# Gate and up projections as seven block products of 256 tokens, the gated product kept in float32 until the down projection, the norm factor of up applied behind it

## The chip, the core and the metric

The kernel runs on one core of a Trainium2 chip. That core has a matrix engine (TensorE, PE in the rows; its weight loads stand apart as PEld), VectorE (DVE), ScalarE (ACT), GpSimd (POOL), a queue engine that issues transfers (SyncE, SP), and sixteen DMA engines. What counts is device time of one call in microseconds; lower is better. TensorE has two clock levels, 1.2 and 2.4 GHz; the profile gives the granted clock as a share of the higher one.

## The reference

One layer of a hybrid encoder on 512 tokens of width 1024 with 16 meta tokens: two attention branches, merged and projected, then a SwiGLU block, then a last norm. Only the second half matters here:

```
x = x + merged @ w_o
h = rmsnorm(x, ffn_norm)
x = x + (jax.nn.silu(h @ w_gate) * (h @ w_up)) @ w_down
h = rmsnorm(x, final_norm)
return h[:, N_META:]
```

`w_gate` and `w_up` are 1024 x 2816, `w_down` is 2816 x 1024, all float32. The norm divides each token by the root of its mean square, so its factor is one number per token and can be applied after a projection as well as before it.

## The kernel before

Features lie on the 128 partitions, tokens along the free axis: `x1` is 8 tiles of 128 features by 512 tokens. A float32 product is made of three matmuls (`mm3`): every operand is split into a high part in float32r (a cast on ScalarE) and the rest (a subtraction on VectorE), and high x high, high x low and low x high are added up in PSUM. Each matmul has a 128x128 weight tile and 512 tokens, and each has its own weight load.

The last part of the program, `phase_b`, has these stages on TensorE, one after the other without barriers:

- `pn` (32 x 3 matmuls), the attention branch that is left, and the merge; `po` (64 x 3), the output projection, whose result is added to `x1`, scaled by the norm's weight and split into `xgh`, `xgl`;
- gate and up: 22 passes, one for each block f of 128 of the 2816 columns. A pass runs 8 x 3 matmuls for gate and 8 x 3 for up, and then `glu` (lines 971 to 979): VectorE multiplies gate by the norm factor R2, ScalarE applies silu, VectorE multiplies up by R2 and the two with each other, and the product is split at once into `gh[:, f]`, `gl[:, f]`. The sum of squares that R2 needs is complete only when the stage begins, so its small matmuls (`ms`, line 183) and the matmul that spreads it over the partitions (`rp`, line 886) stand in passes 0 and 1;
- down: 8 output blocks m, each 22 x 3 matmuls (`pdn`) over all blocks of `gh`, `gl`. The last block is done in two halves of 256 tokens (`pdh`, line 919), so that the final norm and the store of one half run beside the other.

Weights come in pieces of 512 KB in the order of `wplan`; `wnext` (line 124) keeps up to four pieces loaded and up to two split. `wraw` has three buffers, `whi` and `wlo` two each. The order on each engine is not the order of the text: a scheduler lists the instructions by readiness under a model of their cost, and each engine then works through its list strictly in that order, waiting on semaphores.

Of the kernel before, what the change touches and what calls it, by code (L numbers as in the profile page):

```python
# [10 lines left out]
F32 = mybir.dt.float32  # L11
# [23 lines left out]
NF = D_FF // P  # L35
EPS = 1e-6
# [32 lines left out]
class Kernel:  # L69
# [9 lines left out]
    def wplan(self):  # L79
# [58 lines left out]
    def mm3(self, outs, wh, wl, rhs, start, stop):  # L138
        nc = self.nc
        n = len(outs)  # L140
        for i in range(n):
            nc.tensor.matmul(outs[i], wh, rhs[i][0], start=start, stop=False)  # L142
        for i in range(n):
            nc.tensor.matmul(outs[i], wh, rhs[i][1], start=False, stop=False)  # L144
        for i in range(n):
            nc.tensor.matmul(outs[i], wl, rhs[i][0], start=False, stop=stop)  # L146
# [662 lines left out]
    def phase_b(self, sA2):  # L809
        tc, nc, a = self.tc, self.nc, self.a  # L810
        with ExitStack() as top:
            self.pjp = top.enter_context(tc.tile_pool(name="pjb", bufs=8, space=PSUM))
            X = top.enter_context(tc.tile_pool(name="X", bufs=1, side="right"))
            x1 = X.tile([P, KT, T], F32, name="x1")
            bt = top.enter_context(tc.tile_pool(name="bt", bufs=1, side="right"))
            sX = ExitStack()
            XG = sX.enter_context(tc.tile_pool(name="XG", bufs=1, side="right"))
            xgh = XG.tile([P, KT, T], F32R, name="xgh")
            xgl = XG.tile([P, KT, T], F32R, name="xgl")
            for m in range(KT):  # L820
                nc.gpsimd.dma_start(x1[:, m], a["x"][m][:, :T])
            sM = ExitStack()
            M = sM.enter_context(tc.tile_pool(name="M", bufs=1))
            mh = M.tile([P, KT, T], F32R, name="mh")
            ml = M.tile([P, KT, T], F32R, name="ml")
            m2 = self.m2
            for m in range(KT):
# [12 lines left out]
                self.split(mh[:, m], ml[:, m], m2[:, m])  # L840


            ssq = bt.tile([P, T], F32, name="ssq2", tag="ssq", bufs=1)
            for m in range(KT):
                wh, wl = self.wnext()
                po = self.pj("po")
                for k in range(KT):
                    self.mm3([po], wh[:, k], wl[:, k], [(mh[:, k], ml[:, k])], k == 0, k == KT - 1)
                nc.vector.tensor_tensor(out=x1[:, m], in0=x1[:, m], in1=po, op=ALU.add)
                nc.scalar.activation(xgh[:, m], x1[:, m], AF.Copy, scale=self.g2[:, m:m + 1])  # L850
                nc.vector.scalar_tensor_tensor(out=xgl[:, m], in0=x1[:, m], scalar=self.g2[:, m:m + 1],
                                               in1=xgh[:, m].bitcast(F32), op0=ALU.mult, op1=ALU.subtract)
                self.sum_sq(bt, ssq, x1[:, m], m, KT)
            sM.close()
            sA2.close()


            sG = ExitStack()
            G = sG.enter_context(tc.tile_pool(name="G", bufs=1))
            gh = G.tile([P, NF, T], F32R, name="gh")  # L860
            gl = G.tile([P, NF, T], F32R, name="gl")
            R2 = bt.tile([P, T], F32, name="R2")
            held = []
            for f in range(NF):
                pgu = []
                for j in range(2):
                    wh, wl = self.wnext()
                    ps = self.pj("pf")
                    for k in range(KT):
                        self.mm3([ps], wh[:, k], wl[:, k], [(xgh[:, k], xgl[:, k])], k == 0, k == KT - 1)  # L870
                        if f == 0 and j == 1 and k < 4:
                            if k == 0:
                                ms = self.pj("ms2")
                                msg = self.mean_sq(ms, ssq, P, 4, self.ones_d)
                            next(msg)
                    pgu.append(ps)
                if f == 0:
                    y = self.rsqrt(ms[:, 0:4], EPS)
                    dg = bt.tile([P, T], F32, name="dg", tag="t0", bufs=3)
                    self.diag(dg.rearrange("p (c q) -> p c q", c=4), y, P, 4)  # L880
                held.append((f, pgu))
                if f == 0:
                    continue
# [4 lines left out]
                while held:  # L888
                    self.glu(bt, R2, gh, gl, *held.pop(0))
# [180 lines left out]
```

## Time and profile before

| | us |
|---|---|
| median of three runs (lowest, highest) | 783.49 (781.88, 784.15) |
| the profiled execution | 784.85 |
| its span, first to last instruction | 783.1 |
| gate and up, first matmul to the first of down (408.47 to 649.69) | 241.2 |
| down, without its last block (649.69 to 754.41) | 104.7 |
| last block of down | 18 |
| behind the last matmul of down | 10.6 |

The profile is one execution. TensorE's busy time is the union of its matmuls' durations; each duration contains the time that a matmul takes to drain, which overlaps with the next one, so the duration of one (391 ns) is longer than the spacing of two starts. Spacings are read from starts.

### The profile page before, as it was taken

To read this page: it belongs to the slowest core of one execution; us is meant where nothing else is said; L and a number is where in the kernel's file an instruction comes from. 1 tells how busy PE (TensorE), PEld (TensorE's weight loads), DVE (VectorE), ACT (ScalarE), POOL (GpSimd) and SP (SyncE) were. 2 spreads that over 40 slices of the span, in tenths; PEclk is the share of its full clock that TensorE was granted. 3 is DMA by queue.
4 is the path that set the end of the run, shared out by engine and by line. 5 is a ranking of instruction groups with operands and counts; after the bars stand their busy time and mean duration, and the time that the engine had idled before them with its cause. 6 is when DMAs were issued, how large, how long until landed. Compare 5 with 4: busy or idle time off the path is not lost.

```text
span 783.1 us, 10564 instructions
## 1 busy us (share of the span) xinstructions
PE 768.4 (98%) x4002; PEld 654.0 (84%) x4002; DVE 457.5 (58%) x888; ACT 310.4 (40%) x522; POOL 58.3 (7%) x141
## 2 busy tenths in 40 slices
PE   7999999999999999999999999999999999999995
PEld 5899889989999888878888888888888888888884
DVE  5778898798788866657453644444444445222314
ACT  6246555555545547424341523223232233222311
POOL 2030110110011000020220000000000000000100
PEclk8999999999999999999999999999999999999997
DMA  7474644444463411353323222323323235332313
GB/s 261 130 193 130 167 117 110 128 124 129 113 170 107 107 70 63 100 185 111 104 84 108 81 100 88 108 87 101 100 89 108 88 94 173 104 95 78 108 37 107
DMA packets 31970, 89.20 MB, mean 114 GB/s; under 512 B 4208, under 2 KB 6272, under 8 KB 31920
## 3 DMA queue, kind: packets, MB, share of 16 engines
q1 hardware_dynamic: 29952, 84.41, 35.5%
q0 software_dynamic: 1136, 3.34, 1.5%
q10 hardware_dynamic: 832, 0.79, 0.3%
q8 instruction: 31, 0.51, 0.3%
q14 instruction: 19, 0.16, 0.1%
HBM read 71.45 MB, written 2.10 MB: 94 GB/s over the span
## 4 chain that ended last, share of the span: by engine, by line
PE 92%; DVE 4%; DMA 2%; SPq 1%; issue 1%; ACT 0%; DVEq 0%; ACTq 0%
PE pf L142 10%; PE pf L144 10%; PE pf L146 10%; PE pdn L146 4%; PE pdn L142 4%; PE pdn L144 4%; PE pg L142 4%; PE pg L144 4%; PE pg L146 4%; PE s L515 2%; PE po L146 2%; PE po L144 2%; PE po L142 2%; PE pq L142 2%; PE pq L144 2%; PE pq L146 2%
## 5 line engine op out<-in xcount | busy, mean ns | idle before, releaser
L119 ACT CAST whi<-wraw 128x1024 fp32r<-128x1024 f32 (+2 forms) x123 | 126.9, 1032 | 297.4 <-issue 108.3
L120 DVE TENSOR_TENSOR wlo<-wraw,whi 128x1024 fp32r<-128x1024 f32 (+2 forms) x123 | 147.4, 1198 | 91.7 <-ACT whi L119 87.1
L142 PE MATMUL pf<-xgh,whi 128*128 128x512 f32 x352 | 137.7, 391 | 0.0
L144 PE MATMUL pf<-xgl,whi 128*128 128x512 f32 x352 | 137.0, 389 | 0.0
L146 PE MATMUL pf<-xgh,wlo 128*128 128x512 f32 x352 | 137.0, 389 | 0.0
L142 PEld LDWEIGHTS pf<-xgh,whi 128*128 128x128 f32 x352 | 66.1, 188 | 13.9 <-issue 0.2
L146 PEld LDWEIGHTS pf<-xgh,wlo 128*128 128x128 f32 x352 | 66.1, 188 | 13.9
L144 PEld LDWEIGHTS pf<-xgl,whi 128*128 128x128 f32 x352 | 66.1, 188 | 13.6 <-issue 0.2
L142 PE MATMUL pdn<-gh,whi 128*128 128x512 f32 x154 | 59.9, 389 | 0.0
L144 PE MATMUL pdn<-gl,whi 128*128 128x512 f32 x154 | 59.9, 389 | 0.0
L146 PE MATMUL pdn<-gh,wlo 128*128 128x512 f32 x154 | 59.9, 389 | 0.0
L977 DVE TENSOR_TENSOR u<-pf,R 128x512 f32<-128x512 f32 x22 | 15.2, 691 | 65.6 <-PE pf L146 65.6
L142 PE MATMUL pg<-xh,whi 128*128 128x512 f32 x128 | 52.7, 411 | 0.4 <-DVE vt L381 0.4
L144 PE MATMUL pg<-xl,whi 128*128 128x512 f32 x128 | 50.6, 396 | 0.0
L146 PE MATMUL pg<-xh,wlo 128*128 128x512 f32 x128 | 50.2, 392 | 0.0
L989 POOL TENSOR_TENSOR ssq<-ssq,sq 128x512 f32<-128x512 f32 x11 | 19.4, 1761 | 376.5 <-ACT sq L988 376.5
L975 DVE TENSOR_TENSOR s<-pf,R 128x512 f32<-128x512 f32 x22 | 15.2, 690 | 42.1 <-PE pf L146 42.1
L156 ACT CAST ath<-tp 128x256 fp32r<-128x256 f32 (+1 forms) x48 | 20.5, 443 | 42.3 <-PE tp L639 22.0
L146 PEld LDWEIGHTS pdn<-gh,wlo 128*128 128x128 f32 x154 | 28.9, 188 | 6.1
L144 PEld LDWEIGHTS pdn<-gl,whi 128*128 128x128 f32 x154 | 28.9, 188 | 6.1
L142 PEld LDWEIGHTS pdn<-gh,whi 128*128 128x128 f32 x154 | 28.9, 188 | 5.9
L142 PE MATMUL pk<-xh,whi 128*128 128x256 f32 (+1 forms) x128 | 29.2, 306 | 2.7 <-ACT xh L246 2.7
(222 smaller groups left out, 1497.9 us busy)
## 6 DMA issues: line engine op xcount, KB each, us to landing
wraw<-in_w_in_dram SPq DMA_DIRECT2D x39, 512.0 KB, 3.5
wraw<-in_w_gate_dram SPq DMA_DIRECT2D x22, 512.0 KB, 3.2
wraw<-in_w_up_dram SPq DMA_DIRECT2D x22, 512.0 KB, 3.2
kd<-khl SPq DMA_DIRECT2D x32, 264.0 KB, 4.1
wraw<-in_w_down_dram SPq DMA_DIRECT2D x16, 512.0 KB, 3.5
qs<-qhl SPq DMA_DIRECT2D x32, 128.0 KB, 2.9
wraw<-in_w_o_dram SPq DMA_DIRECT2D x8, 512.0 KB, 3.3
wraw<-in_w_down_dram SPq DMA_DIRECT2D x8, 384.0 KB, 3.1
```

The lines of the kernel that those rows point to most:

```text
L119: nc.scalar.copy(hi[:, k:k + h], raw[:, k:k + h])
L120: eng.tensor_tensor(out=lo[:, k:k + h], in0=raw[:, k:k + h], in1=hi[:, k:k + h].bitcast(F32), op=ALU.subtract)
L142: nc.tensor.matmul(outs[i], wh, rhs[i][0], start=start, stop=False)
L144: nc.tensor.matmul(outs[i], wh, rhs[i][1], start=False, stop=False)
L146: nc.tensor.matmul(outs[i], wl, rhs[i][0], start=False, stop=stop)
L156: self.nc.scalar.copy(hi, src)
L515: nc.tensor.matmul(sc[:, r0:r1], qs[:, q], kd[:, p, r0:r1], start=p == 0, stop=p == 1)
L975: nc.vector.tensor_tensor(out=s, in0=pgu[0], in1=R2, op=ALU.mult)
L977: nc.vector.tensor_tensor(out=u, in0=pgu[1], in1=R2, op=ALU.mult)
L989: (nc.gpsimd if m < n - 1 else nc.vector).tensor_tensor(out=ssq, in0=ssq, in1=sq, op=ALU.add)
```

## The change

Three things change, all in `phase_b`.

**Gate and up.** The two outputs of a pass (gate and up), the two halves of the 1024 inputs and the two halves of the tokens make a product of 2x2 blocks by 2x2 blocks. Eight block products (each 4 x 3 matmuls of 256 tokens) are replaced by Strassen's seven, in Winograd's form. The token side needs seven operands for the whole stage: `x_operands` makes them from `x1` with four sums per pair of blocks and splits them (`xbh`, `xbl`). The weight side needs seven operands per pass: `f_prep` makes four sums (`W[:, 1]`, `V[:, 1]`, and two in `G`) and splits all seven, in four casts and four subtractions. `f_products` runs the seven products into three PSUM tiles pa, pb and pc, where sums that share a product go on accumulating; ScalarE copies what must be kept from an intermediate stage into `c1` and `c2`. Pass 0 runs its products in another order. `glu` adds the parts.

**The norm factor of up** (here negated, `nR2`) is left out of `glu` and multiplied onto the output of down, where it is the same number per token: in `end` and in `dense`.

**The gated product** `g` is kept in float32 and split only when down begins, all 22 blocks then. Down runs blocks m = 0 and 1 together over k, and its weights are split ahead into a ring of seven slots (`d_ahead`), which lies in the memory of the token operands. `x` is loaded again into the memory of `m2`, each block as soon as it is split.

```
+    def f_prep(self, f):
...
+        g = hilo(G, [P, 2, 4, P], ("whi", "wlo"), 2, self.wp)
+
+        nc.vector.tensor_tensor(out=W[:, 1], in0=V[:, 0], in1=W[:, 0], op=ALU.add)
+        w = hilo(W, [P, 2, 4, P], ("fwh", "fwl"), 2, F)
+
+        nc.vector.tensor_tensor(out=V[:, 1], in0=W[:, 1], in1=G[:, 0], op=ALU.add)
+        s = hilo(V[:, 1], [P, 4, P], ("fsh", "fsl"), 1, F)
+
+        nc.vector.tensor_tensor(out=G, in0=G, in1=V, op=ALU.add)
+        d = hilo(G, [P, 2, 4, P], ("fdh", "fdl"), 1, F)
...
+    def f_products(self, G, xbh, xbl, f, ssq):
...
+        def product(out, i, first, last):
+            wh, wl = wt[i]
+            for k in range(4):
+                self.mm3([out], wh[:, k], wl[:, k], [(xbh[:, i, k], xbl[:, i, k])],
+                         first and k == 0, k == 3, skip_group_check=True)
...
+        def p2():
+            product(blo, PB21, False, True)
+
+        def p4():
+            product(pc, PT4, True, True)
+            nc.scalar.copy(c2[:, 0], pc)
+
+        def p6():
+            product(pa, PT2, False, False)
+            nc.scalar.copy(c1[:, 1], pa)
+        product(pa, PB11, True, False)
+        nc.scalar.copy(c1[:, 0], pa)
+        product(bhi, PT1, True, False)
+        nc.scalar.copy(c2[:, 1], bhi)
+        for part in (p2, p6, p4) if f == 0 else (p4, p6, p2):
+            part()
+        product(bhi, PB22, False, True)
+        product(pa, PT3, False, True)
+        return c1, c2, pa, pb
...
-        nc.vector.tensor_tensor(out=s, in0=pgu[0], in1=R2, op=ALU.mult)
+        nc.vector.tensor_tensor(out=s, in0=c1.rearrange("p j n -> p (j n)"), in1=pb, op=ALU.add)
+        nc.vector.tensor_tensor(out=s, in0=s, in1=nR2, op=ALU.mult)
         nc.scalar.activation(s, s, AF.Silu)
-        nc.vector.tensor_tensor(out=u, in0=pgu[1], in1=R2, op=ALU.mult)
-        nc.vector.tensor_tensor(out=u, in0=s, in1=u, op=ALU.mult)
-        self.split(gh[:, f], gl[:, f], u)
+        nc.vector.tensor_tensor(out=u.rearrange("p (j n) -> p j n", j=2),
+                                in0=pa.unsqueeze(1).to_broadcast([P, 2, H]), in1=c2, op=ALU.add)
+        g.append(G.tile([P, T], F32, name="g", tag="g", bufs=NF + 1))
+        nc.vector.tensor_tensor(out=g[f], in0=s, in1=u, op=ALU.mult)
...
+            gh = [GH.tile([P, T], F32R, name=f"gh{k}") for k in range(NF)]
...
+            for k in range(NF):
+                gl.append(G.tile([P, T], F32R, name="gl", tag="g", bufs=NF + 1))
+                self.split(gh[k], gl[k], g[k])
...
+            def end(m):
+                t = bt.tile([P, T], F32, name="t", tag="t0", bufs=3)
+                nc.vector.tensor_tensor(out=t, in0=pd[m], in1=nR2, op=ALU.mult)
+                nc.vector.tensor_tensor(out=x1[:, m], in0=x1[:, m], in1=t, op=ALU.subtract)
...
-                nc.vector.tensor_tensor(out=x1[:, m, t], in0=x1[:, m, t], in1=pd, op=ALU.add)
+                u = bt.tile([P, T], F32, name="u", tag="t0", bufs=3)[:, :H]
+                nc.vector.tensor_tensor(out=u, in0=pd, in1=nR2[:, t], op=ALU.mult)
+                nc.vector.tensor_tensor(out=x1[:, m, t], in0=x1[:, m, t], in1=u, op=ALU.subtract)
```

How the lists of the engines move at the two places that matter. First VectorE in the middle of gate and up, before: one pass is these six rows (u and s of `glu`, the split of the product, two splits of weight pieces).

```order
L977 TENSOR_TENSOR u<-pf,R_4552 128x512
L978 TENSOR_TENSOR u<-s,u 128x512
L120 TENSOR_TENSOR wlo<-wraw,whi 128x1024
L157 TENSOR_TENSOR gl<-u,gh 128x512
L975 TENSOR_TENSOR s<-pf,R_4552 128x512
L120 TENSOR_TENSOR wlo<-wraw,whi 128x1024
```

The same place after the change: one pass is eleven rows (fW, fV and fG are the sums of weights; fwl, fsl, wlo and fdl are the low parts of the seven weight operands; nR is the norm factor).

```order
L1038 TENSOR_TENSOR fW<-fV,fW 128x512
L1103 TENSOR_TENSOR g<-s,u 128x512
L1041 TENSOR_TENSOR fV<-fW,fG 128x512
L155 TENSOR_TENSOR fwl<-fW,fwh 128x1024
L155 TENSOR_TENSOR fsl<-fV,fsh 128x512
L155 TENSOR_TENSOR wlo<-fG,whi 128x1024
L1097 TENSOR_TENSOR s<-c_5561,pb 128x512
L1044 TENSOR_TENSOR fG<-fG,fV 128x1024
L155 TENSOR_TENSOR fdl<-fG,fdh 128x1024
L1098 TENSOR_TENSOR s<-s,nR_4625 128x512
L1100 TENSOR_TENSOR u<-pa,c_5562 128x512
```

Five rows more per pass: two of 1024 elements and three of 512. On TensorE a pass goes from 48 matmuls of 512 tokens to 84 of 256.

Second, the seam from gate and up to down. TensorE before: the last matmuls of up (pf) and the first of down.

```order
L142 MATMUL pf<-xgh,whi 128x512
L144 MATMUL pf<-xgl,whi 128x512
L146 MATMUL pf<-xgh,wlo 128x512
L142 MATMUL pdn<-gh,whi 128x512
L144 MATMUL pdn<-gl,whi 128x512
L146 MATMUL pdn<-gh,wlo 128x512
```

TensorE after: the last product of gate and up (pa) and then down's blocks 0 and 1 in turn (gh_7396 is the high part of block 0 of the gated product).

```order
L140 MATMUL pa<-xb,fdh 128x256
L142 MATMUL pa<-xb,fdh 128x256
L144 MATMUL pa<-xb,fdl 128x256
L140 MATMUL pdn<-gh_7396,dhi 128x512 x2
L142 MATMUL pdn<-gl,dhi 128x512
L144 MATMUL pdn<-gh_7396,dlo 128x512
```

VectorE after, at the seam: the last pass's `glu` (s, s, u, g) stands ahead of the first low part of the gated product.

```order
L155 TENSOR_TENSOR dlo<-draw,dhi 128x1024
L1097 TENSOR_TENSOR s<-c_7294,pb 128x512
L1098 TENSOR_TENSOR s<-s,nR_4625 128x512
L1100 TENSOR_TENSOR u<-pa,c_7295 128x512
L1103 TENSOR_TENSOR g<-s,u 128x512
L155 TENSOR_TENSOR gl<-g,gh_7396 128x512
L155 TENSOR_TENSOR gl<-g,gh_7397 128x512
```

ScalarE after, at the seam: the first two high parts, then the silu of the last pass, then the other high parts.

```order
L154 CAST dhi<-draw 128x1024
L154 CAST gh_7396<-g 128x512
L154 CAST gh_7397<-g 128x512
L1099 ACTIVATE s<-s 128x512
L154 CAST gh_7398<-g 128x512
L154 CAST gh_7399<-g 128x512
```

The first cast gh_7396 waits for the last matmul of gate and up, whose weights lay in the memory of `gh`; before, `gh` and `gl` of block 0 were complete 21 passes earlier.

## Rows read from the trace of the kernel before

**Rows 1.** The page: the span, busy time of the engines, and the granted clock in 40 slices (tenths).

```profile
span 783.1 us, 10564 instructions
PE 768.4 (98%) x4002; PEld 654.0 (84%) x4002; DVE 457.5 (58%) x888; ACT 310.4 (40%) x522; POOL 58.3 (7%) x141
...
PEclk8999999999999999999999999999999999999997
```

**Rows 2.** The page: the chain of work that ended last, by engine.

```profile
PE 92%; DVE 4%; DMA 2%; SPq 1%; issue 1%; ACT 0%; DVEq 0%; ACTq 0%
```

**Rows 3.** Windows by stage: busy time of each engine with the number of instructions, then granted clock, DMA share, GB/s. The third is gate and up.

```profile
364.86:408.34 43.48, 43.48 (x194) 36.01 (x193) 21.67 (x26) 17.46 (x24) 10.75 (x6) 1.00 0.30 97
408.34:649.75 241.41, 241.41 (x1069) 199.64 (x1068) 113.18 (x145) 74.17 (x92) 0.00 (x0) 1.00 0.30 96
649.75:754.41 104.66, 104.66 (x463) 86.66 (x462) 33.17 (x33) 31.68 (x37) 8.61 (x5) 1.00 0.35 106
```

**Rows 4.** Timeline of TensorE in the middle of gate and up (start, duration): a matmul and the 48th behind it.

```profile
500.09 0.39 PE L142 MATMUL pf<-xgh,whi 128*128 128x512 f32 x1
...
510.97 0.39 PE L142 MATMUL pf<-xgh,whi 128*128 128x512 f32 x1
```

**Rows 5.** Timeline of TensorE in the last block of down, matmuls of 256 tokens each with its own weights: the first and the last of 56 in a row.

```profile
758.46 0.28 PE L142 MATMUL pdh<-gh,hi 128*128 128x256 f32 x1
...
765.06 0.28 PE L144 MATMUL pdh<-gl,hi 128*128 128x256 f32 x1
```

**Rows 6.** Groups of instructions by line: matmuls of gate and up (one of three lines), and weight loads of the last block of down.

```profile
L142 PE MATMUL pf<-xgh,whi 128*128 128x512 f32 x352 | 137.7, 391 | 0.0
...
L142 PEld LDWEIGHTS pdh<-gh,hi 128*128 128x128 f32 x44 | 8.4, 192 | 0.1
```

**Rows 7.** Timeline of VectorE in the middle of gate and up (start, duration): one pass.

```profile
519.33 0.69 DVE L977 TENSOR_TENSOR u<-pf,R 128x512 f32<-128x512 f32 x1 [3.31 <-PE pf L146]
520.13 0.69 DVE L978 TENSOR_TENSOR u<-s,u 128x512 f32<-128x512 f32 x1
520.74 1.22 DVE L120 TENSOR_TENSOR wlo<-wraw,whi 128x1024 fp32r<-128x1024 f32 x1
521.88 0.68 DVE L157 TENSOR_TENSOR gl<-u,gh 128x512 fp32r<-128x512 f32 x1
524.77 0.69 DVE L975 TENSOR_TENSOR s<-pf,R 128x512 f32<-128x512 f32 x1 [2.21 <-PE pf L146]
```

**Rows 8.** Groups of ScalarE by line and shape: the cast of a weight piece, silu, the cast of the product, a copy of 256 elements out of PSUM.

```profile
L119 ACT CAST whi<-wraw 128x1024 fp32r<-128x1024 f32 x114 | 119.8, 1051 | 273.5 <-issue 108.3 <-PE pf L144 73.2 <-PE pdn L144 48.3
L156 ACT CAST gh<-u 128x512 fp32r<-128x512 f32 x22 | 13.7, 626 | 13.3 <-DVE u L978 13.3
L976 ACT ACTIVATE s<-s 128x512 f32<-128x512 f32 x22 | 13.7, 625 | 0.0
...
L439 ACT COPY raw<-pk 128x256 f32<-128x256 f32 x4 | 1.5, 364 | 0.5 <-PE pk L146 0.5
```

**Rows 9.** Timeline of ScalarE: a cast of 512 elements and a cast of 1024 directly behind it; a cast of 1024 and the silu directly behind it.

```profile
359.05 0.62 ACT L156 CAST mh<-m 128x512 fp32r<-128x512 f32 x1 [1.36 <-DVE m L839]
359.57 1.05 ACT L119 CAST whi<-wraw 128x1024 fp32r<-128x1024 f32 x1
...
502.83 1.05 ACT L119 CAST whi<-wraw 128x1024 fp32r<-128x1024 f32 x1 [3.11 <-PE pf L144]
503.79 0.62 ACT L976 ACTIVATE s<-s 128x512 f32<-128x512 f32 x1
```

**Rows 10.** Groups of VectorE by line and shape: operations of 256 and of 768 elements.

```profile
L157 DVE TENSOR_TENSOR atl<-tp,ath 128x256 fp32r<-128x256 f32 x32 | 12.9, 415 | 2.1 <-ACT ath L156 1.8
...
L120 DVE TENSOR_TENSOR wlo<-wraw,whi 128x768 fp32r<-128x768 f32 x7 | 6.7, 958 | 24.0 <-ACT whi L119 24.0
```

**Rows 11.** What TensorE waited for in the whole span: total, times, longest.

```profile
PE pk L142 <- ACT xh L246: 2.7, 1, 2.7
PE rp L944 <- DVE dg L189: 1.7, 1, 1.7
...
PE pn L142 <- ACT whi L119: 0.9, 1, 0.9
```

**Rows 12.** Windows around two waits of TensorE and around the 0.9 us wait (columns as in rows 3; the clock is the third number from the right).

```profile
7.00:8.00 1.00, 0.56 (x5) 0.35 (x3) 0.00 (x0) 0.00 (x0) 0.00 (x0) 1.00 0.79 248
...
10.00:10.30 0.30, 0.00 (x0) 0.00 (x0) 0.30 (x2) 0.30 (x2) 0.00 (x0) 0.50 1.07 415
16.60:16.80 0.20, 0.20 (x3) 0.20 (x3) 0.20 (x1) 0.20 (x1) 0.00 (x0) 0.50 0.50 205
16.80:17.00 0.20, 0.20 (x3) 0.20 (x3) 0.20 (x2) 0.20 (x1) 0.00 (x0) 0.94 0.35 143
342.00:370.00 28.00, 27.12 (x121) 22.32 (x120) 21.85 (x30) 10.03 (x13) 4.25 (x8) 1.00 0.46 158
774.40:774.60 0.20, 0.00 (x0) 0.00 (x0) 0.07 (x1) 0.10 (x1) 0.00 (x0) 0.95 0.00 0
774.60:774.80 0.20, 0.00 (x0) 0.00 (x0) 0.17 (x2) 0.00 (x0) 0.00 (x0) 0.50 0.00 0
```

**Rows 13.** The chain behind the last matmul of down, first step (start, duration).

```profile
772.48 0.43 DVE x L921
```

**Rows 14.** Transfers of gate's weights: KB each, median us from issue to landing.

```profile
wraw<-in_w_gate_dram SPq DMA_DIRECT2D x22, 512.0 KB, 3.2
```

More of the change, by code (lines that the diff above doesn't have):

```diff
@@ L35 @@
 NF = D_FF // P
+H = T // 2
+PB11, PB21, PB22, PT1, PT3, PT2, PT4 = range(7)
 EPS = 1e-6
@@ L863, in phase_b @@
+            g = []
+            nR2 = G.tile([P, T], F32, name="nR2")
             held = []
             for f in range(NF):
[L865 to L876, printed above, removed]
+                if f + 2 < NF:
+                    self.f_load(f + 2)
+                if f + 1 < NF:
+                    self.f_prep(f + 1)
+                held.append((f, self.f_products(G, xbh, xbl, f, ssq)))
@@ new lines, in phase_b @@
+            sF.close()
+            GH = top.enter_context(tc.tile_pool(name="GH", bufs=1))
+            gh = [GH.tile([P, T], F32R, name=f"gh{k}") for k in range(NF)]
+            gl = []
+            ring = [XB.tile([P, nxb + 64], F32R, name="wring", tag=t)[:, :7 * 8 * P]
+                    .rearrange("p (i k n) -> p i k n", i=7, k=8) for t in ("xbh", "xbl")]
+            self.ring = ring
+            ssq = bt.tile([P, T], F32, name="ssq3", tag="ssq", bufs=1)
+            pieces = [(0, 0), (1, 0), (0, 1), (1, 1), (0, 2), (1, 2)]
@@ new lines, in phase_b, with block @@
+            pieces += [(m, p) for m in range(2, KT) for p in range(3)]
+            self.dp, self.dload, self.dsplit = pieces, 0, 0
+            self.draw, self.dw = {}, {}
+            self.d_ahead(2)
+            pd = {}
+            for k in range(NF):
+                gl.append(G.tile([P, T], F32R, name="gl", tag="g", bufs=NF + 1))
+                self.split(gh[k], gl[k], g[k])
+            def block(m, k):
+                wh, wl = self.dw[m, k // 8]
+                self.mm3([pd[m]], wh[:, k % 8], wl[:, k % 8], [(gh[k], gl[k])], k == 0, k == NF - 1)
@@ L897, in phase_b @@
+            end(0)
+            end(1)
+            for m in range(2, KT - 1):
+                pd[m] = self.pj("pdn")
                 for k in range(NF):
                     if k % 8 == 0:
-                        wh, wl = self.wnext()
-                    self.mm3([pd], wh[:, k % 8], wl[:, k % 8], [(gh[:, k], gl[:, k])], k == 0, k == NF - 1)
-                nc.vector.tensor_tensor(out=x1[:, m], in0=x1[:, m], in1=pd, op=ALU.add)
-                self.sum_sq(bt, ssq, x1[:, m], m, KT - 1)
-                nc.scalar.activation(x1[:, m], x1[:, m], AF.Copy, scale=self.g3[:, m:m + 1])
@@ L904, in phase_b @@
-            wq = []
-            for p in range(3):
-                raw = W2.tile([P, 8, P], F32, name=f"raw{p}")
-                hi = W2.tile([P, 8, P], F32R, name=f"hi{p}")
-                lo = W2.tile([P, 8, P], F32R, name=f"lo{p}")
-                n = min(8, NF - 8 * p)
-                nc.sync.dma_start(raw[:, :n], a["w_down"][KT - 1][:, 8 * p:8 * p + n])
-                self.split(hi[:, :n], lo[:, :n], raw[:, :n])
-                wq.append((hi, lo))
+                        self.d_ahead(3 * m + k // 8 + (2 if m < KT - 2 else 4))
@@ L913, in phase_b @@
+                    block(m, k)
+                end(m)
+            self.d_ahead(len(pieces))
             m = KT - 1
-            H = T // 2
             def dense(t):
```

155 lines of the change are left out of this document (114 added, 41 removed).

## The prediction

> **What bounds the kernel now.** I read the page first: TensorE is busy 98% of the span, the chain that ended last is 92% TensorE, and the granted clock is full in all slices but the first and the last [rows 1, 2]. The list of TensorE's waits holds only a few us, none of them in the second half except the last norm [rows 11]. So an edit is worth what it does to TensorE's stream; work on the other engines costs nothing until it makes TensorE wait. Then the windows by stage: in gate and up TensorE is busy for all of 241.4 us, VectorE for 113 and ScalarE for 74 [rows 3]. That is room on VectorE for about as much work again, and the change takes nearly all of it. That makes the order of work as important as its sum.
>
> **Matmuls of gate and up.** The duration of a matmul (391 ns [rows 6]) says nothing on throughput; its spacing does. 48 matmuls of 512 tokens take 510.97 - 500.09 = 10.88 us, 226.7 ns each [rows 4]. Matmuls of 256 tokens, each with a weight load of its own, stand in the last block of down: 55 spacings in 765.06 - 758.46 = 6.60 us, 120.0 ns each [rows 5]. That is more than half of 226.7: solving the two gives 0.417 ns per token, and 13.3 ns that every matmul costs whatever its width. Before: 22 x 48 x 0.2267 = 239.4 us. After: 22 x 7 x 12 = 1848 matmuls x 0.120 = 221.8 us. **Gain 17.6 us**, not an eighth of the stage (29.9 us): an eighth of the tokens streamed is worth 28.2, and 792 matmuls more give 10.5 back. Weight loads of 192 ns [rows 6] already overlap at a spacing of 120 ns, so loading more often costs no more than this. The small matmuls of the norm (ms, rp) stay, and I leave them at zero.
>
> The Trainium skill, in "TensorE: Matmul & The Clock Gate", section "Back-to-back issue gap", gives the spacing of an isolated matmul at full clock as its columns divided by 2.4 GHz plus 2.5 ns, so 109 and 216 ns. An estimate by that page would be a gain of 26 us. The rows above measure both widths in this kernel and do not agree with it.
>
> **VectorE and ScalarE inside a pass.** These must fit in the new pass, 84 x 0.120 = 10.08 us. Two operations of 512 elements back to back start 0.61 us apart, one of 1024 takes 1.14 us until the next starts (520.13, 520.74, 521.88 [rows 7]). The new pass has seven of 512 and four of 1024: 7 x 0.61 + 4 x 1.14 = 8.83 us, 88% of the pass. ScalarE has three casts of 1024 (0.96 apart [rows 9]), one of 512 and a silu (0.63 each), four copies of 256 out of PSUM (0.36 each [rows 8]): 5.6 us.
>
> Fitting as a sum isn't enough, since each engine works its list in order. I follow one pass from its first matmul at 0; the seven products end at multiples of 1.44. ScalarE's casts overwrite weights that TensorE has just used: fwh after the third product (4.3 us), fsh after the fourth (5.8), whi after the fifth (7.2), fdh after the seventh (10.1). VectorE follows each: fwl at 5.4, fsl at 6.6, wlo at 8.3, then s (needs the sixth product, 8.8) at 9.4, fG at 10.0, fdl at 11.1 when its cast is done, then s, u, fW, g, fV to 15.2, where the next fwl waits until 15.4. So VectorE gets round once per pass with about 1.2 us of waiting. What TensorE needs comes early: fsl and fdl about 5 us ahead of their products, fwl and wlo more than a pass ahead. The tightest are ScalarE's copies, which must leave PSUM before the next product adds to it: the copy of the fourth product ends near 6.7, and the seventh starts at 8.64, 1.9 us later. Stall per pass taken as 0; bounds 0 to 0.1 us (2.2 us in all). Transfers: still 1 MB per pass, now as one of 512 KB (3.2 us to land [rows 14]) and two of 256 KB, each issued over 6 us before its use. Cost 0.
>
> **The seam into gate and up.** Five of the seven token operands need the last block of po, and the sums of the first weights are made in the po stage too, where VectorE is busy for only half the time [rows 3]. From the end of the seventh block (5.44 us before the stage begins, 24 x 0.2267) VectorE's list up to the sum of squares is: three operations of 1024, one weight-sum of 1024 (4 x 1.14), four of 512 (2.4), four of 256 (0.35 each by [rows 10], less the overlap of 0.07), one of 768 (0.88), 9.3 us, and 0.7 of handing over: it ends 4.6 us into the stage. TensorE has 33 matmuls ahead of it (3.96 us), then waits. **Cost 0.6 us**; bounds 0 and 3, the latter if the parts of passes 0 and 1 that follow, in which VectorE has hardly a margin, are late as well.
>
> **The seam into down.** Before there was no wait here. Now the first cast of the gated product starts 0.2 us after TensorE's last product would have let the next matmul start, and takes 0.63 [rows 8]; two matmuls run (0.45), and the third needs gl of block 0. In its way stand on ScalarE a second cast (0.52 [rows 9]) and the silu (0.63), on VectorE the multiplication g (0.61), then gl itself (0.69): 0.2 + 0.52 + 0.52 + 0.63 + 0.1 + 0.61 + 0.69 = 3.3 us. TensorE idles 3.3 - 0.45 = **2.85 us**, bounds 2 (the silu hands over earlier) and 4. Behind it gl comes every 0.61 us for 1.36 us of matmuls. ScalarE makes 22 casts and the silu before the first ring piece: 0.2 + 23 x 0.52 + 0.96 = 13.1 us; TensorE asks for it at 3.3 + 0.45 x 2 + 7 x 1.36 = 13.7. At full clock the second piece, 0.96 later, makes it wait up to 0.4 us; at a lower clock not at all.
>
> **The clock.** A wait of 2.7 us at the start of the program let the granted clock fall to half; the matmuls restarted behind 10.30 and ran at half until about 16.8, 6.5 us that cost 3.25 [rows 11, 12]. In the tail, with a few tiny matmuls in between, it fell 2.1 us after the last large one [rows 12, 13]. A wait of 0.9 us did nothing [rows 11, 12]. The wait into down is 2.85 us in two pieces, so it is nearest to the first. **Cost 3.25 us**; bounds 0 and 3.25.
>
> **Down and tail.** The output blocks gain one operation of 512 on VectorE, which is mostly idle there, so nothing. The second half of the last block has it in the open: one more operation of 256, **0.45 us** (0.43 and the hand-over [rows 13]). Loading x again into m2 issues eight transfers from GpSimd one by one, each needed about 20 us later: nothing.
>
> **Sum.** The profiled execution took 784.85. 784.85 - 17.6 + 0.6 + 2.85 + 3.25 + 0.45 = 774.4. That execution lies 1.36 above the median of the runs, so the median should be **773.0 us**.
>
> **Rivals.**
> - *The clock holds at the seam into down* (the wait is split by two matmuls). Then 3.25 goes and 0.4 for the ring comes: 770.2. For it: the 0.9 us wait did nothing. Against: 2.85 of 3.3 us idle.
> - *The seams cost their upper bounds* (3, 4, 3.25, 0.5), with 0 to 2.2 for small stalls in the passes: 777 to 779.5. For it: VectorE has hardly a margin in passes 0 and 1.
> - *VectorE takes TensorE's place as the bound of the passes, and the kernel gets slower.* Its list holds four low parts behind ScalarE's casts. If three of those casts stand in the open (1.05 each [rows 8]), a pass takes 8.83 + 3.15 = 11.98 us, and 22 x (11.98 - 10.88) = +24 in place of -17.6: 815. It decides from 2.05 us of such waiting per pass on (10.88 - 8.83). Against it: by the walk through a pass they wait for TensorE's own progress, about 1.2 us in all.
> - *Matmuls of 256 tokens don't keep 120 ns* when seven products alternate among three PSUM tiles and transfers run beside them. At 125 ns the gain is 8.4 and the time 782; at 129.5 it is gone. Against: every matmul of [rows 5] changes its weights too.
> - *The 13.3 ns shrink in the new stream* to the few ns of the page: 8.6 us less than forecast, 764.4. That page is the Trainium skill's, named above; no row points there.
>
> **How the numbers follow.** Forecast 0.49, clock holds 0.27, seams at their bounds 0.12, 125 ns or more 0.05, VectorE the bound 0.06, the smaller overhead 0.01. Faster or slower counts beyond 0.3% of 783.49 (2.35 us), about what a measurement of this kernel can tell from no change. Faster: 0.49 + 0.27 + 0.12 + 0.01 = 0.89; same 0.05 (the 125 ns); slower 0.06. The range takes in the forecast and its two neighbours: below, the clock holds and the seams come at their lower bounds (770.2 - 0.6 - 0.85 - 0.4 = 768.3), and a run may lie 1.6 below its median (783.49 - 781.88), so 767; above, 779.5, and 0.7 for the same reason (784.15 - 783.49), so 780.
>
> **What would show it.** In the profile of the changed kernel: pa, pb and pc start 0.120 us apart and a pass takes 10.08 us; VectorE is busy for nearly the whole of gate and up, yet TensorE's list of waits names no line of the passes; two waits are new, one for the sum of squares near the start of gate and up (under 1 us) and one for gl at the start of down (two pieces, 2.85 us); behind it matmuls of 512 tokens are 0.44 us apart for some us at granted clock 0.5. I am wrong if the passes show waits on VectorE or ScalarE each time, if the spacing is not 0.120, or if the seams hold more than 7 us.

## The result, and the profile after

The changed kernel takes 772.44 us, median of four runs (770.94 to 773.11), the kernel before 783.80 beside it (781.88 to 784.15): ratio 0.9857, 95% interval 0.9834 to 0.9881. 773.0 was forecast. The profiled execution took 773.11, 11.74 less than that of before (784.85).

The page after, its lines for [rows 1, 2]: span, busy time, clock, chain.

```profile
span 771.3 us, 12598 instructions
PE 748.6 (97%) x4794; PEld 674.1 (87%) x4794; DVE 575.6 (75%) x1053; ACT 379.7 (49%) x669; POOL 55.3 (7%) x141
...
PEclk8999999999999999999998999999999999999998
...
PE 85%; DVE 9%; DMA 2%; issue 1%; ACT 1%; SPq 0%; DVEq 0%; ACTq 0%
```

TensorE still bounds, but VectorE has got 9% of the chain, and the clock has a dent in its 22nd slice, at the start of gate and up and not at the start of down.

Windows by stage, to compare with [rows 3]: the output projection, gate and up, the same without its first 20 us, the start of down.

```profile
364.86:408.14 43.28, 43.28 (x192) 35.84 (x191) 36.58 (x50) 25.54 (x40) 8.29 (x8) 1.00 0.44 141
...
408.14:633.20 225.06, 221.26 (x1859) 219.97 (x1857) 199.13 (x257) 125.48 (x203) 2.26 (x1) 0.98 0.31 99
428.20:633.20 205.00, 204.99 (x1752) 204.30 (x1750) 182.22 (x226) 115.75 (x187) 0.00 (x0) 1.00 0.33 105
633.20:650.32 17.12, 13.48 (x57) 10.39 (x57) 15.22 (x23) 14.72 (x26) 0.00 (x0) 1.00 0.10 25
```

From 428.20 to the end of gate and up TensorE idles 0.01 us in 205, with VectorE busy for 89%: the passes run as forecast. What TensorE loses in these two stages lies in the first 20 us of gate and up and the first 17 of down. VectorE, about half busy in the output projection before, is now 85% busy there (36.58 of 43.28).

TensorE's waits after, those over 1 us that are new or longer than in [rows 11]. The third is in the tail, 1.0 before; the shorter ones stand in brackets in the timelines below. A wait at the start of the program, 2.7 before and 3.1 here, is left out: in the traces of the other runs it is anything from 2.2 to 4.0.

```profile
PE ms L181 <- DVE ssq L1137: 2.2, 1, 2.2
...
PE pdn L142 <- DVE gl L155: 1.6, 1, 1.6
PE ms L181 <- ACT sq L949: 1.5, 1, 1.5
...
PE pdn L144 <- DVE wring L155: 1.3, 1, 1.3
```

The first seam on TensorE's timeline (start, duration; in brackets the idle time before and its releaser):

```profile
411.53 0.28 PE L144 MATMUL pc<-xb,fwl 128*128 128x256 f32 x1
412.66 0.38 PE L140 MATMUL pc<-xb,fwh 128*128 128x256 f32 x1 [0.86 <-ACT xb L154]
413.81 0.38 PE L142 MATMUL pc<-xb,fwh 128*128 128x256 f32 x1 [0.76 <-DVE xb L155]
414.03 0.28 PE L144 MATMUL pc<-xb,fwl 128*128 128x256 f32 x1
416.48 1.87 PE L181 MATMUL ms<-ones_d,ssq 128*128 128x1 f32 x8 [2.17 <-DVE ssq L1137]
418.20 0.56 PE L140 MATMUL pa<-xb,whi 128*128 128x256 f32 x1
418.56 0.41 PE L142 MATMUL pa<-xb,whi 128*128 128x256 f32 x1
418.77 0.41 PE L144 MATMUL pa<-xb,wlo 128*128 128x256 f32 x1
```

Three waits, and behind them matmuls some 0.213 apart: the granted clock is 0.50 in the window from 418.20 to 422.40, and 1.00 from 422.80.

VectorE and GpSimd at the end of the output projection's work, four operations of VectorE and one of GpSimd that runs beside the third:

```profile
407.69 0.42 DVE L1010 TENSOR_TENSOR xt<-xg 128x256 f32<-128x256 f32 x1
408.03 1.22 DVE L1044 TENSOR_TENSOR fG<-fG,fV 128x1024 f32<-128x1024 f32 x1
409.17 1.78 DVE L155 TENSOR_TENSOR xb<-xg,xb 128x512 fp32r<-128x512 f32 x1
...
413.67 0.68 DVE L854 TENSOR_TENSOR m<-m,po 128x512 f32<-128x512 f32 x1
...
408.06 2.33 POOL L1137 TENSOR_TENSOR ssq<-ssq,sq 128x512 f32<-128x512 f32 x1 [5.56 <-ACT sq L1136]
```

A subtraction of 512 elements takes 0.68 elsewhere, here 1.78. Each of GpSimd's six additions in this stage has such an operation beside it, 0.97 to 1.10 us too long. The addition of the eighth block's output to x (line 854), whose matmuls ended near 408.3, starts only at 413.67.

In the kernel before, GpSimd makes the same six additions and no operation of VectorE is held up. Each addition starts just behind an operation of VectorE there, and it is the addition that gets longer, 1.78 to 1.84 in place of the 1.28 to 1.30 that it takes where it starts first:

```profile
378.08 0.75 DVE L851 SCALAR_TENSOR_TENSOR xgl<-x,vec,xgh 128x512 fp32r<-128x512 f32 x1
...
378.13 1.84 POOL L989 TENSOR_TENSOR ssq<-ssq,sq 128x512 f32<-128x512 f32 x1 [31.10 <-ACT sq L988]
```

In both kernels the one that starts later pays. After the change VectorE's list is so dense that the next operation with two inputs always starts behind an addition.

The start of down: VectorE, then TensorE.

```profile
634.93 0.69 DVE L1103 TENSOR_TENSOR g<-s,u 128x512 f32<-128x512 f32 x1 [0.38 <-ACT s L1099]
635.53 12.56 DVE L155 TENSOR_TENSOR gl<-g,gh 128x512 fp32r<-128x512 f32 x16
648.01 1.22 DVE L155 TENSOR_TENSOR wring<-draw,wring 128x1024 fp32r<-128x1024 f32 x1
```

```profile
632.91 0.27 PE L144 MATMUL pa<-xb,fdl 128*128 128x256 f32 x1
633.89 0.73 PE L140 MATMUL pdn<-gh,dhi 128*128 128x512 f32 x2 [0.71 <-ACT gh L154]
636.28 0.50 PE L142 MATMUL pdn<-gl,dhi 128*128 128x512 f32 x1 [1.65 <-DVE gl L155]
...
647.59 0.40 PE L142 MATMUL pdn<-gl,wring 128*128 128x512 f32 x1
649.28 0.50 PE L144 MATMUL pdn<-gh,wring 128*128 128x512 f32 x1 [1.29 <-DVE wring L155]
```

Sixteen subtractions in 12.56 us are 0.79 apart, not 0.61 as in [rows 7]; the ring's first piece stands behind them. The clock stays at 1.00 in this execution.

**Where the 11.8 us of span went**, by these rows (a gap between two starts counts less the usual spacing):

| step | forecast | measured |
|---|---|---|
| matmuls of gate and up | -17.6 | 22 x 9.80 - 239.4 = -23.8 |
| stalls in the steady passes | 0 | 0 |
| waits at the first seam | +0.6 | 1.01 + 1.03 + 0.10 + 2.33 = +4.5 |
| half clock at the first seam | 0 | 20 matmuls 2.1, ms 0.8: +2.9 |
| wait into down | +2.85 | 0.86 + 1.94 = +2.8 |
| ring | 0 to 0.4 | 1.69 - 0.23 = +1.5 |
| half clock in down | +3.25 | 0 |
| tail | +0.45 | +0.2 (its wait 0.46 longer, the last stores 0.3 shorter) |

The rest, +0.1, is small shifts elsewhere. Half clock in down is 0 in this execution only; experiment 5 comes back to it. The sum of the forecast is -10.45, the measured one -11.8.

### The profile page after: what moved, and what is told of

It reads as the page before. It is cut to its first block, busy times and chain, and to the rows that moved or that the text cites. A ratio compares the mean times of both kernels' runs of the same rounds, so it can differ in the third digit from the quotient of the medians.

```text
span 771.3 us, 12598 instructions
## 1 busy us (share of the span) xinstructions
PE 748.6 (97%) x4794; PEld 674.1 (87%) x4794; DVE 575.6 (75%) x1053; ACT 379.7 (49%) x669; POOL 55.3 (7%) x141
## 4 chain that ended last, share of the span: by engine, by line
PE 85%; DVE 9%; DMA 2%; issue 1%; ACT 1%; SPq 0%; DVEq 0%; ACTq 0%
PE pdn L144 4%; PE pdn L140 4%; PE pdn L142 4%; PE pa L140 4%; PE pa L144 4%; PE pb L140 4%; PE pg L140 4%; PE pa L142 4%; PE pb L142 4%; PE pb L144 4%; PE pg L144 4%; PE pg L142 4%; PE s L513 2%; PE pv L140 2%; PE pv L142 2%; PE pv L144 2%
## 5 line engine op out<-in xcount | busy, mean ns | idle before, releaser
L117 ACT CAST whi<-wraw 128x1024 fp32r<-128x1024 f32 (+1 forms) x57 | 58.9, 1033 | 56.9 <-PE pd L142 13.1
L118 DVE TENSOR_TENSOR wlo<-wraw,whi 128x1024 fp32r<-128x1024 f32 (+1 forms) x57 | 68.5, 1201 | 17.2 <-ACT whi L117 16.9
L144 PE MATMUL pdn<-gh,wring 128*128 128x512 f32 x138 | 53.8, 390 | 1.3 <-DVE wring L155 1.3
L140 PE MATMUL pdn<-gh,wring 128*128 128x512 f32 x138 | 53.8, 390 | 0.0
L142 PE MATMUL pdn<-gl,wring 128*128 128x512 f32 x138 | 53.7, 389 | 0.0
L155 DVE TENSOR_TENSOR wring<-draw,wring 128x1024 fp32r<-128x1024 f32 (+1 forms) x22 | 24.7, 1126 | 28.8 <-ACT wring L154 28.8
L155 DVE TENSOR_TENSOR wlo<-fG,whi 128x1024 fp32r<-128x1024 f32 x22 | 26.9, 1224 | 14.4 <-ACT whi L154 14.4
L144 PEld LDWEIGHTS pdn<-gh,wring 128*128 128x128 f32 x138 | 25.9, 188 | 7.1 <-DVE wring L155 1.7
L140 PEld LDWEIGHTS pdn<-gh,wring 128*128 128x128 f32 x138 | 25.9, 188 | 5.6 <-ACT wring L154 0.2
L142 PEld LDWEIGHTS pdn<-gl,wring 128*128 128x128 f32 x138 | 25.9, 188 | 5.3
L155 DVE TENSOR_TENSOR fwl<-fW,fwh 128x1024 fp32r<-128x1024 f32 x22 | 26.9, 1225 | 3.1 <-ACT fwh L154 3.1
L144 PEld LDWEIGHTS pg<-xh,wlo 128*128 128x128 f32 x128 | 24.0, 188 | 5.2
L621 ACT ACTIVATE en<-en,m 128x272 f32<-128x272 f32 x32 | 16.7, 522 | 24.1 <-DVE m L619 23.8
```

Source lines behind the costliest of these rows:

```text
L117: nc.scalar.copy(hi[:, k:k + h], raw[:, k:k + h])
L118: eng.tensor_tensor(out=lo[:, k:k + h], in0=raw[:, k:k + h], in1=hi[:, k:k + h].bitcast(F32), op=ALU.subtract)
L155: self.nc.vector.tensor_sub(lo, src, hi.bitcast(F32))
L621: x = nc.scalar.activation(e[:, :n], e[:, :n], AF.Exp, bias=m, scale=-1.0, accum_out=l[:, 0:1])
```

## Experiments

Questions: why the matmuls were faster than 120 ns, whether the two seams cost what the rows say and why, how near VectorE is to becoming the bound, and what the width alone costs.

**1. Start addresses of the streamed operands.** The changed kernel starts the token operands 32 bytes past a multiple of 64, in a line that the diff above didn't show. The first run undoes that alone.

```
-            xbh, xbl = (t[:, 8:8 + nxb].rearrange("p (i k n) -> p i k n", i=7, k=4) for t in xbt)
+            xbh, xbl = (t[:, :nxb].rearrange("p (i k n) -> p i k n", i=7, k=4) for t in xbt)
```

> The changed kernel, with the token operands of gate and up moved down by 32 bytes, so that each starts at a multiple of 64 bytes in its partition (in the changed kernel 32 bytes past one); nothing else. Theory A, the start address of the streamed operand sets the fixed part of a matmul: the 256-token matmuls of the passes go from 0.1167 to 0.120 us apart, as those of the last block of down, whose operands start at multiples of 64; a pass takes 10.08 us in place of 9.80, 22 x 84 x 0.0033 = 6.1 us more, 778.5 in all. Theory B, the stream of seven products or the passes' PSUM tiles give the shorter spacing: 0.1167 stays and the time stays at 772.4.

777.59 us, ratio 0.9928 (0.9909 to 0.9948): 5.2 more. The first matmul of one pass and of the next, in the changed kernel and in this run:

```profile
505.63 0.28 PE L140 MATMUL pa<-xb,whi 128*128 128x256 f32 x1
...
515.43 0.28 PE L140 MATMUL pa<-xb,whi 128*128 128x256 f32 x1
```

```profile
505.57 0.28 PE L140 MATMUL pa<-xb,whi 128*128 128x256 f32 x1
...
515.65 0.28 PE L140 MATMUL pa<-xb,whi 128*128 128x256 f32 x1
```

9.80 against 10.08 us: 0.1167 and 0.1200 per matmul. Nothing but the address differs, so it is the cause, and theory A holds. The opposite move, on the operands of the first projections and of the output projection (`xh`, `xl`, `mh`, `ml` up by 8 elements, as `[:, 8:8 + ...]`):

> The changed kernel, with the streamed operands of the first projections (normalised input) and of the output projection moved up by 32 bytes, so that they start 32 bytes past a multiple of 64, as those of gate and up do; nothing else. Theory A (start address): 512-token matmuls of these stages go from 0.2267 to 0.2233 us apart, 256-token ones from 0.120 to 0.1167; 1344 + 192 matmuls x 0.0033 = 5.1 us less if TensorE is the bound there throughout, at least 3: 767.3 to 769.5. Theory B (the shorter spacing belongs to the passes of gate and up): no change, 772.4.

774.01, ratio 0.9872 (0.9855 to 0.9888): not faster. 512-token matmuls of the output projection went from 0.2267 to 0.2353 us apart (191 spacings) and those of the first projections from 0.230 to 0.233, while 256-token ones of the first projections went from 0.119 to 0.117 (nine spacings). Theory A holds for 256 tokens and has the wrong sign for 512. Two more places, on the passes (256 tokens) and the output projection (512):

> The changed kernel, with the token operands of gate and up (256-token matmuls) and those of the output projection (512-token matmuls) starting 16 bytes past a multiple of 64. Measured so far: at multiples of 64 the spacing is 0.1200 and 0.2267 us, at 32 past them 0.1167 and 0.2353. Theory A, what counts is that a start does not fall on a multiple of 64: 0.1167 and about 0.235 here too. Theory B, the 32 bytes themselves count: 0.1200 and 0.2267 here, or values between.

> As the run before, but both kinds of operands start 64 bytes further on than in the run at multiples of 64 (an odd multiple of 64 bytes in place of an even one). If the place within 64 bytes is all that counts: 0.1200 and 0.2267. If it is the place within a longer stretch (128 bytes or more): other values, as at 32.

| operands start at | 256 tokens, us apart | 512 tokens, us apart |
|---|---|---|
| as in the first run | 0.1200 | 0.2267 |
| 16 bytes on | 0.1167 | 0.2311 |
| 32 bytes on | 0.1167 | 0.2353 |
| 64 bytes on | 0.1178 | 0.2304 |

Single runs, 770.63 and 772.65; a row's first number comes from some 1800 matmuls of one trace, its second from 191. The place within 64 bytes isn't all that counts, since 64 bytes on differs too. Each shift makes the narrow matmul cheaper and the wide one dearer. Why is open. (For the wide ones `mh` and `ml` were also made 64 or 128 bytes longer, so `ml` may have moved by more than the row says; the operands of the passes moved by just that.)

**2. The seam into down**, opened: the high parts take over the weight buffers one by one, and no low part is written over the block read just before it.

```
+            for tag, bufs, n in (("fV", 2, 2), ("fW", 2, 2), ("fwh", 2, 2), ("fwl", 2, 2),
+                                 ("fsh", 1, 1), ("fsl", 1, 1), ("fdh", 1, 2), ("fdl", 1, 2)):
+                for _ in range(bufs):
+                    t = self.F.tile([P, n, T], F32R, name="gh", tag=tag, bufs=bufs)
+                    gh += [t[:, i] for i in range(n)]
...
-                gl.append(G.tile([P, T], F32R, name="gl", tag="g", bufs=NF + 1))
+                tag, bufs = (("c1", 2), ("c2", 2))[k] if k < 2 else ("g", NF)
+                gl.append(G.tile([P, T], F32R, name="gl", tag=tag, bufs=bufs))
```

> The changed kernel, with the seam into down opened: the high parts of the gated product take over the buffers of the weights one by one instead of waiting for the whole pool, the low parts are not written directly behind the block read before (gl of block k goes over the float32 product of block k-3 instead of k-1), and the last product has a buffer of its own, so that some nine blocks are split within the last pass. Theory A, TensorE waits at the seam for the first low part, and for the ring because each subtraction waits for the end of the one before (0.795 us apart): the waits for gh and gl (0.7 + 1.65) vanish, subtractions that follow each other directly come 0.61 apart, the ring's wait of 1.3 shrinks below 0.8; 3 to 4 us less, 768.5 to 769.5. Rival: the split parts delay the weights of the last pass, or the ring piece waits for the same reason wherever the parts stand, and less than 1 us is won, 771.5 to 772.5.

768.06, ratio 0.9805 (0.9786 to 0.9824), 4.4 less than the changed kernel, as much as the waits (2.8) and the ring (1.5) together. No `pdn` is left in TensorE's waits, and down without its last block takes 105.22 us in place of 108.47. The profiled execution is the longest of the four, 771.07: in it TensorE's waits at the first seam are 5.6 us in place of 4.5, and its clock is low for longer behind them. Whether the edit causes that is open. VectorE, within the last pass:

```profile
629.18 5.50 DVE L155 TENSOR_TENSOR gl<-g,gh 128x512 fp32r<-128x512 f32 x9
634.60 1.22 DVE L155 TENSOR_TENSOR dlo<-draw,dhi 128x1024 fp32r<-128x1024 f32 x1
```

Nine in 5.50 us are 0.60 apart, and so are ten more behind the seam, where they stood before (6.10 us from 639.94). In the changed kernel each subtraction wrote where the one before had read, and so waited for its end; that was the 0.79.

**3. Sums of squares on VectorE** in the output projection.

```
-            (nc.gpsimd if m < n - 1 else nc.vector).tensor_tensor(out=ssq, in0=ssq, in1=sq, op=ALU.add)
+            (nc.gpsimd if m < n - 1 and n < KT else nc.vector).tensor_tensor(out=ssq, in0=ssq, in1=sq, op=ALU.add)
```

> The changed kernel, with the six sums of squares of the output-projection stage on VectorE instead of GpSimd; nothing else. Theory A, GpSimd's addition holds up a VectorE operation that runs beside it by 1.08 us, more than the addition costs on VectorE itself (0.60): VectorE ends its list 2 to 4 us earlier, TensorE's waits in the first pass of gate and up (0.86, 0.76 and 2.2) shrink to half or less, the clock drop behind them shrinks or goes; 3 to 6 us less, 766.5 to 769.5. Rival: the long operations have another cause, VectorE only gets 6 x 0.60 = 3.6 us more to do, and the wait grows: 773 to 775.

770.08, ratio 0.9826 (0.9812 to 0.9841): 2.4 less, the sign of theory A but under its range. VectorE has six operations more in the stage, and gets through earlier:

```profile
406.05 0.68 DVE L1137 TENSOR_TENSOR ssq<-ssq,sq 128x512 f32<-128x512 f32 x1
406.65 0.68 DVE L155 TENSOR_TENSOR xb<-xg,xb 128x512 fp32r<-128x512 f32 x1
...
409.06 0.68 DVE L854 TENSOR_TENSOR m<-m,po 128x512 f32<-128x512 f32 x1
```

No operation is long any more. The seventh block's addition to x starts at 403.17 in place of 405.96, right behind its matmuls and not 3.1 us later, and the last at 409.06 in place of 413.67. TensorE's waits at the seam fell to 1.1 and 1.0, but the clock still fell behind them, and some 27 matmuls ran at half of it; that is where the expectation had too large a gain.

**4. Both together**, with the last sum of squares listed ahead of the last block's operands (`if m == KT - 1: self.sum_sq(...)` ahead of `x_operands`).

> The changed kernel with the opened seam into down (768.1 alone) and the sums of squares on VectorE (770.1 alone) together, and the last sum of squares listed ahead of the last block's operands, so that TensorE's small matmuls on it come without a wait. Theory A, the two lie at different places and add up: 772.4 - 4.4 - 2.4 = 765.7, and about 1 us less for the wait for the sum of squares (1.0 in the run with the sums on VectorE alone): 764.7; if the clock then holds at the first seam, where some 20 matmuls ran at half of it, about 2.5 less again, 762.2. Rival: VectorE's list is only shifted, TensorE waits as long for the token operands instead of the sum: 765.7 or more.

764.19 (762.42 to 766.00), ratio 0.9746 (0.9729 to 0.9763), faster than the changed kernel and than either edit alone. The profiled execution:

```profile
412.83 0.39 PE L142 MATMUL pc<-xb,fwh 128*128 128x256 f32 x1 [1.06 <-DVE xb L155]
413.05 0.28 PE L144 MATMUL pc<-xb,fwl 128*128 128x256 f32 x1
413.43 1.05 PE L181 MATMUL ms<-ones_d,ssq 128*128 128x1 f32 x8
414.34 0.36 PE L140 MATMUL pa<-xb,whi 128*128 128x256 f32 x1
414.55 0.28 PE L142 MATMUL pa<-xb,whi 128*128 128x256 f32 x1
```

One wait of 1.06 is left, the clock holds, and this execution took 762.63. The mean clock of the five runs is 0.989 to 0.994, highest in the two fastest (762.42 and 762.63), so it seems to fall at the seam in some; only this one has a trace.

**5. How near VectorE is to the bound.** Once the norm factor of up is put back into the pass:

```
+        nc.vector.tensor_tensor(out=u, in0=u, in1=nR2, op=ALU.mult)
```

> The changed kernel with one of its parts undone: up is multiplied by the norm factor inside the pass again (one VectorE operation of 512 more per pass, 0.60), and not behind down. Theory A, VectorE's 0.9 us of waiting per pass is slack that the operation fills: the passes stay at 9.80 us, 0.45 us are won back in the tail and up to 0.6 lost at the seam into down: 772 to 773. Rival, VectorE's waits for ScalarE's casts stay as long: a pass takes 9.80 + 0.5 = 10.3 us, 22 x 0.5 = 11 us more, 783.

772.31, ratio 0.9859 (0.9841 to 0.9878): the same as the changed kernel, theory A. (The block's contribution enters x with the opposite sign in this run; operations and their number are as described.) Its passes take 9.80 us as well. Leaving the factor out of the pass saves no time here. Then two sums made twice:

```
-        nc.vector.tensor_tensor(out=W[:, 1], in0=V[:, 0], in1=W[:, 0], op=ALU.add)
+        for _ in range(2 if f > 2 else 1):
+            nc.vector.tensor_tensor(out=W[:, 1], in0=V[:, 0], in1=W[:, 0], op=ALU.add)
...
-        nc.vector.tensor_tensor(out=V[:, 1], in0=W[:, 1], in1=G[:, 0], op=ALU.add)
+        for _ in range(2 if f > 2 else 1):
+            nc.vector.tensor_tensor(out=V[:, 1], in0=W[:, 1], in1=G[:, 0], op=ALU.add)
```

> The changed kernel, in which two weight sums of each pass from the fourth on are simply made twice over (two VectorE operations of 512 more per pass, 1.20 us; the result is the same). VectorE's operations then sum up to 8.74 + 1.20 = 9.94 us per pass by their spacing, more than the 9.80 of TensorE. Theory A, VectorE's waiting gives way to work and it becomes the bound only by its sum: passes of 9.94 to 10.1 us, 3 to 6 us more, 775 to 778. Rival, the waits for ScalarE's casts (0.9 per pass) are a fixed part of its round: passes of 10.85, 19 x 1.05 = 20 us more, 792.

773.64, ratio 0.9868 (0.9854 to 0.9883): 1.2 more, under both theories' range and too little to tell from the changed kernel. VectorE's round, from one fwl to the next:

```profile
519.96 1.21 DVE L155 TENSOR_TENSOR fwl<-fW,fwh 128x1024 fp32r<-128x1024 f32 x1
...
529.91 1.21 DVE L155 TENSOR_TENSOR fwl<-fW,fwh 128x1024 fp32r<-128x1024 f32 x1
```

9.95 us without a wait in between, where TensorE's pass takes 9.80. The trace shows what happens to the difference. From the fifth pass to the twelfth TensorE keeps 9.80, and the time by which the low part fsl is ready ahead of its product shrinks by 0.15 per pass, from 4.82 us to 3.74. From the thirteenth on it stays near 3.66, and passes 13 to 21 take 89.8 us, 1.6 more than at 9.80. There TensorE waits for a copy out of PSUM that stands behind the silu on ScalarE, and the silu waits for VectorE:

```profile
548.19 0.63 ACT L1101 ACTIVATE s<-s 128x512 f32<-128x512 f32 x1 [1.15 <-DVE s L1100]
548.73 0.35 ACT L1084 COPY c<-pa 128x256 f32<-128x256 f32 x1
...
549.14 0.39 PE L140 MATMUL pa<-xb,fsh 128*128 128x256 f32 x1
```

So theory A has the mechanism, and its price was too high because the lead is used up first. Without the two sums VectorE's round is 9.95 - 1.20 = 8.75, so its margin in the changed kernel is 1.05 us per pass. With 1.20 more it becomes the bound, late in the stage.

This execution shows something else. The waits into down are as in the changed kernel (0.86 and 1.94), but behind them the granted clock fell: matmuls are 0.427 apart. The window from 638.50 to 641.00 here, and one from 634.50 to 637.00 in the run with operands at 16 bytes, whose waits are the same again:

```profile
638.50:641.00 2.50, 2.50 (x7) 1.98 (x6) 2.15 (x4) 2.50 (x6) 0.00 (x0) 0.50 0.00 0
...
634.50:637.00 2.50, 2.50 (x7) 1.94 (x6) 2.12 (x4) 2.50 (x6) 0.00 (x0) 0.50 0.00 0
```

In both the wait for the ring is gone, since TensorE gets to it later, and down without its last block takes 108.50 us, against 108.47 in the changed kernel. Of the seven traces with these two waits, five keep the clock and these two don't. (In the run with the norm factor inside, the second wait is 0.45 longer, and the clock fell there too.)

**6. The width alone**, in the kernel before: each gate and up matmul as two of 256 tokens. (The two halves share a PSUM bank and the values of gate and up come out different; the time is that of the same stream.)

```
-                        self.mm3([ps], wh[:, k], wl[:, k], [(xgh[:, k], xgl[:, k])], k == 0, k == KT - 1)
+                        hs = (slice(0, T // 2), slice(T // 2, T))
+                        self.mm3([ps[:, t] for t in hs], wh[:, k], wl[:, k],
+                                 [(xgh[:, k, t], xgl[:, k, t]) for t in hs], k == 0, k == KT - 1,
```

> The kernel before, with nothing of the change but the width: every gate and up matmul of 512 tokens is made as two of 256 with the same weights, whose operands start at multiples of 64 bytes (eight block products of 256 tokens in place of Strassen's seven). Theory A, a matmul costs 0.417 ns per token and 13.3 ns beside, whoever it belongs to: 96 x 0.120 = 11.52 us per pass in place of 10.88, 22 x 0.64 = 14.1 us more, 798. Rival, a second matmul with the weights of the one before goes without the fixed part: 48 x (0.2267 + 0.1067 - 0.1067) = 10.88, no change, 783.8.

798.32, ratio 1.0176 (1.0162 to 1.0191), 14.2 more than before, theory A to 0.1 us:

```profile
500.00 0.40 PE L142 MATMUL pf<-xgh,whi 128*128 128x256 f32 x2
500.24 0.40 PE L144 MATMUL pf<-xgl,whi 128*128 128x256 f32 x2
```

Two matmuls per 0.24 us, although the second has the weights of the first. The trace has a weight load for each of them all the same (5058 of both), so what a matmul without one would cost isn't measured. So one product of eight left out gives 798.3 - 22 x 12 x 0.120 = 766.6 if nothing else cost anything, the address 6.1 more: 760.5. What the seams and the tail cost in the table above (4.5 + 2.9 + 2.8 + 1.5 + 0.2 = 11.9) is the distance from there to 772.4, though the table is of one execution and 772.4 a median.

## Why the prediction came out right, and where it didn't

- *What bounds, and the kind of gain*: right. TensorE sets the passes, an eighth of the products saves less than an eighth of the time because every matmul costs something beside its tokens, and experiment 6 gives the price per matmul that I solved for.
- *Matmuls of gate and up*: the term is mis-sized, -17.6 in place of -23.8. The 120.0 ns came from [rows 5], whose operands start elsewhere in memory; I took a fixed 13.3 ns for a property of the matmul, and it was 10.0 in this stream. The rival "the 13.3 ns shrink" had the direction and too much of it, and its sum was wrong: it counts only the 792 additional matmuls, although all 1848 of the new stream would shrink; spread over these, 8.6 us less is a fixed part of 8.6 ns, not a few. The Trainium skill, "TensorE: Matmul & The Clock Gate", section "Back-to-back issue gap", would give 109 ns by its formula for an isolated matmul; no pass here averages less than 116.7.
- *Passes*: right. The walk through one pass gave 1.2 us of waiting on VectorE; experiment 5 shows that 1.05 us of it is slack. The rival in which VectorE becomes the bound would have needed more work than that.
- *The seam into gate and up*: the step that failed, 4.5 us of waits where the bounds were 0 and 3. I let VectorE's list begin at the end of the seventh block, "where VectorE is busy for only half the time". That half was the kernel before. In the changed kernel VectorE was 3.1 us late at that point already, because GpSimd's six additions held it up by about 1.1 us each, which they didn't do before; without them (experiment 3) it was on time. The sum of squares came 8.3 us into the stage, not 4.6. The Trainium skill, "SBUF — State Buffer", section "Who interferes with whom", says that a VectorE operation with two inputs in SBUF contends with a GpSimd operation that reads SBUF; the rows agree (1.10 us longer beside an addition, none in experiment 3). It spoke against this change and I didn't weigh it.
- *The seam into down*: the wait is right to 0.1 us, 2.85 against 2.8. The ring is not: I used 0.61 us per subtraction from rows in which no operation depends on the one before.
- *The clock*: in the profiled execution it fell at the other seam and cost about what I said (2.9 against 3.25); that the two prices are near each other is luck. The fall that I forecast behind the waits into down came in two of seven traces, with matmuls 0.427 apart as forecast (0.44), but it costs nothing there beyond what the ring's wait costs without it (108.50 against 108.47). So the step had a possible mechanism and too high a price. In experiment 3 waits of 1.1 and 1.0 with the eight tiny ms matmuls between them and the next product were enough for a fall; in experiment 4's trace one of 1.06, with ms directly behind, was not. The length of a wait alone does not tell, and the same waits don't give the same clock each time.
- *The signs of being wrong*: two that the prediction names came. The spacing was 0.1167 and not 0.120, and the seams held 11.7 us (4.5, 2.8 and 1.5 of waits, 2.9 of half clock), more than 7.
- *The rival of the upper bounds*: its terms add up to 776.6, and 778.8 with the stalls, not 777 to 779.5; only the upper end of the range rests on that.
- The total came out within 0.6 us of the median because errors of 6.2 and 3.25 on one side met 3.9, 2.9 and 1.5 on the other. That is luck.

## What to carry to other kernels

Take a matmul's spacing from rows with the same width and the same placement of the streamed operand, and try the placement itself: 32 bytes were worth 5 us here. Where a change fills an engine, look at the stage ahead of the one it speeds up, since its preparation runs there, and count each GpSimd addition beside a full VectorE as time of VectorE (1.1 us here, 0.60 if VectorE makes it itself). In-place chains of buffers cost 0.18 us per operation; write some blocks away from what was just read. Look at the clock in more than one execution before a price is put on a wait.

## What I had not expected of the hardware

- The start address of the streamed operand changes a float32r matmul's spacing, in opposite directions for 256 tokens (0.1167 to 0.1200) and 512 (0.2267 to 0.2353). Tied to what, weights or banks, is open.
- A GpSimd addition of 512 elements makes a VectorE operation that starts behind it about 1.1 us longer, while VectorE does that addition itself in 0.60. Where the addition starts second, it is the addition that gets longer (1.78 in place of 1.30) and VectorE loses nothing.
- The same two waits (0.86 and 1.94) let the granted clock fall in two traces and not in five, and down took 108.5 us either way, since the wait for the ring goes where the clock falls.
